# Transposing both halves of a head's numerators in one visit, with a second PSUM bank and new planner rules

## The chip, the cores and the metric

The kernel runs on one core of a Trainium2 chip. The metric is the device time of one execution in microseconds, as the median of several runs. A profiled execution gives the trace that is read below. Of the core's engines, TensorE (PE) does matrix products and transposes into PSUM, a small memory of eight banks; VectorE (DVE) and ScalarE (ACT) do elementwise work and empty the banks; GpSimd (POOL) and SyncE (SP) issue DMAs, and ACT issues some too. Each engine runs its own instructions strictly in order, and waits on semaphores for the others.

## The reference

One block of a streaming encoder: 1024 frames with 16 learned tokens ahead of them, model width 1024. Four mLSTM heads and four retention heads are mixed in parallel, then comes a gated MLP with a causal convolution (width 2816). Cut to what matters here:

```python
h = concat(meta, x)                                   # 1040 x 1024
proj = rmsnorm(h) @ w_in                              # q, k, v, output gate, input and forget gates of all heads
# per head (8 heads: 4 mLSTM, 4 retention; q, k 128 wide, v 256 wide), chunk by chunk:
num = (q k^T * decays) v + (q * decay) C              # C is the state carried from chunk to chunk
C   = decay * C + k^T v
h_head = head_norm(num) * g                           # normalised over the head's 256 values
mixed = [sigmoid(o) * h_head | silu(o) * h_head]      # gated, 2048 wide
h = h + mixed @ w_out
h = h + (silu(conv(rmsnorm(h) @ w_up)) * (rmsnorm(h) @ w_gate)) @ w_down
out = rmsnorm(h)
```

## The kernel before

**Products.** Large products are done in a seven-product scheme (Strassen and Winograd). Each operand is split into a high and a low part of type fp32r, and a product is three matmuls: high by high, low by high, high by low (`mm3s`, lines 900 to 902). Everything that belongs to the scan over the chunks (scores `s`, state update `u`, numerator `n`, transposes) is done in plain fp32 instead. So TensorE changes between fp32r and fp32 operands each time the scan gets a turn.

**Stages.** The input is normalised and the first projections made (0 to about 85 us of the trace). Then, head by head in the order 4, 0, 1, 2, 3, 5, 6, 7, come the products of the queries and keys (`q`), the values (`vp`, for a pair of heads; `v` for head 7) and the output gate (`o`). The scan of one head is woven into the products of the following one, up to about 712 us. Then come the output projection (`pw` tiles), the MLP (`up`, `ga`) and the down projection (`pd`). The change touches the weaving between 85 and 712 us.

**The scan of a head.** There are nine chunks (one of 16 tokens, eight of 128), and `scan_a` and `scan_b` handle one each. `scan_a` makes the scores and transposes the keys in the PSUM bank `sA`. `scan_b` makes the state update `u` in the bank `upd` (line 1568), the numerator `n` in the bank `num` (1570, 1572), adds `u` to the state `C` on DVE (1581) and copies the numerator out on ACT (1583). The chunks are grouped in three pieces (`PIECES`: chunks 0 to 3, 4 to 6, 7 and 8). When a piece is normalised (`stats`), its numerators, 256 wide, are transposed in two halves of 128: `half(b)` (line 1623) puts up to four transposes into the one bank `tr` (1629), and DVE multiplies them by the gain and the gate into an SBUF tile `mx` (1637). Three `mx` buffers rotate (1647). For the last piece DVE also copies two columns (1652). Then ACT issues a DMA that stores `mx` to DRAM (1655). Head 7 writes into the operand tiles `wa` of the output projection instead and stores nothing. So a head has six visits of `half`, each between two groups of product matmuls.

**The order of the work is planned when the program is built.** A function `watch` (line 132) sees every instruction, keeps a modelled clock for each engine and pins the order of PE, DVE and ACT between 85 and 712 us. A change between fp32r and fp32 on PE is costed there at 0.1 us (line 178). The products are cut into steps of 12 matmuls for a bank; `slot` (1701) issues a step, and after it takes tasks from the front of a list `side` (the scan, the transposes, the gates), strictly in order, as long as the first one's condition holds. Conditions look at `done`: a key stands there with the modelled time at which it becomes true, and holds when PE's modelled clock has passed it. `half` needs the piece's `z`, the gate's half `sig` and `tr`, which is taken out when the transposes are issued and put back after the multiplication on DVE. A task runs up to its first `yield`; `tick` continues it later. `settle` makes the DMA wait until the planner's clock has passed the modelled end of what came before. `drain` issues what is left of the list at the end of a stage without steps between.

How many tasks a step may take is set by a table `RULES`, with an entry for the seven products of a kind at one of their places, such as `("q", 1)`. Its seven numbers are: how many weight units ahead are treated as near; a slack in us before a waiting task is continued; by how many us DVE or ACT may be ahead of PE before waiting tasks are held back; the same limit for taking new tasks; the most tasks in a step; the order of the queues; the most PE tasks in a step. The clock, the DMA model and the conditions stay as they are.

```python
c += 0.1 * (whole != kindof[0])                       # line 178: the change of operands
tr = ps.tile([P, 512], F32, tag="tr", name=f"tr{h}_{p}_{b}")
mx = mxp.tile([P, WMAX], F32, tag="mx", name=f"mx{h}_{p}_{b}", bufs=3)
yield from settle()
AC.dma_start(mxd[i][:, a0 - MA:e - MA], mx[:, :e - a0])
```

## Time and profile before

| what | before |
|---|---|
| median of 3 runs | 1527.99 us (1526.26 to 1529.33) |
| profiled execution | 1527.2 us, of which the span from first to last instruction is 1525.4 us |
| PE busy | 1489.9 us, 98% of the span |
| DVE busy | 1090.1 us, 71% |
| ACT busy | 755.6 us, 50% |
| granted TensorE clock | 0.994 |

In the timeline a row is one group of instructions: start in us from the span's beginning, duration in us, engine, line, operation, what it writes and reads, shape, count, and in brackets how long its engine sat idle before it and who ended that. PE means matmuls (their ends are modelled, so two rows overlap; the distance of their starts is what they cost). In a table of waits a row is: who waited, for whom, us in total, times, longest. An engine with q behind its name is its sequencer, which issues DMAs.

### The profile page before, as it was taken

The numbers are of one execution on the slowest core, as the hardware profiler recorded it, in microseconds if no ns is written. First come the engines' busy times: TensorE is split into PE (matmuls) and PEld (weight loads), VectorE is DVE, ScalarE is ACT, GpSimd is POOL, SyncE is SP. The second block draws the span as 40 slices with busy tenths as digits, with TensorE's granted clock in tenths as the row PEclk, the third lists the DMA queues.
The fourth block names the chain that finished last, engine by engine and source line by source line (L and its number), as shares of the span: only waits on it lengthen the run. The fifth ranks groups of instructions, "written<-read, shape, count | busy, mean of one in ns | idle before, by whom it ended". The sixth has DMA issues, their size and how long they took to land.

```text
span 1525.4 us, 25488 instructions
## 1 busy us (share of the span) xinstructions
PE 1489.9 (98%) x9929; PEld 1350.0 (88%) x9929; DVE 1090.1 (71%) x2087; ACT 755.6 (50%) x1453; POOL 73.6 (5%) x153
## 2 busy tenths in 40 slices
PE   6999999999999999999999999999999999999997
PEld 6998999999999999986888988999999999888887
DVE  7785868678777677856867787767666666778657
ACT  4465655554655455553454565444444444444443
POOL 1000000000000000000000001222220000000000
PEclk9999999999999999999999999999999999999999
DMA  6022255323532355696333247888772224933313
GB/s 232 8 88 51 86 159 194 111 82 114 186 119 98 125 166 189 195 398 255 111 112 134 80 124 241 197 208 200 189 183 77 83 79 160 369 105 110 97 42 111
DMA packets 104586, 223.81 MB, mean 147 GB/s; under 512 B 10520, under 2 KB 33760, under 8 KB 104288
## 3 DMA queue, kind: packets, MB, share of 16 engines
q1 hardware_dynamic: 89824, 191.68, 37.7%
q0 software_dynamic: 8448, 23.07, 7.6%
q10 hardware_dynamic: 6192, 7.41, 1.4%
q8 instruction: 78, 1.28, 0.4%
q14 instruction: 44, 0.36, 0.1%
HBM read 178.05 MB, written 67.15 MB: 161 GB/s over the span
## 4 chain that ended last, share of the span: by engine, by line
PE 89%; DVE 6%; DMA 2%; ACT 2%; issue 1%; SPq 0%; DVEq 0%; ACTq 0%
PE pdx L902 3%; PE pdx L901 3%; PE pdx L900 3%; PE pup_x L901 2%; PE pup_x L902 2%; PE pga_x L900 2%; PE pup_x L900 2%; PE pga_x L901 2%; PE pga_x L902 2%; PE pdy L902 2%; PE pdy L901 2%; PE pdy L900 2%; PE n L1570 2%; PE pwx L902 2%; PE u L1568 2%; PE pv L940 2%
## 5 line engine op out<-in xcount | busy, mean ns | idle before, releaser
L780 ACT CAST hi_up<-raw_up 128x512 fp32r<-128x512 f32 (+1 forms) x52 | 36.4, 719 | 107.4 <-PE pga_z L901 61.1
L781 DVE TENSOR_TENSOR lo_ga<-fraw_ga,hi_ga 128x512 fp32r<-128x512 f32 (+1 forms) x52 | 41.9, 809 | 37.3 <-ACT hi_ga L780 37.1
L781 DVE TENSOR_TENSOR lo_up<-raw_up,hi_up 128x512 fp32r<-128x512 f32 (+1 forms) x52 | 41.3, 810 | 38.0 <-ACT hi_up L780 37.2
L900 PE MATMUL pup_x<-uh_g,hi_up 128*128 128x256 f32 (+1 forms) x240 | 67.2, 282 | 1.2 <-ACT uh_g L1928 1.2
L901 PE MATMUL pup_x<-ul_g,hi_up 128*128 128x256 f32 (+1 forms) x240 | 67.4, 282 | 0.1
L902 PE MATMUL pup_x<-uh_g,lo_up 128*128 128x256 f32 (+1 forms) x240 | 66.4, 282 | 0.0
L781 DVE TENSOR_TENSOR lo_d<-rd,hi_d 128x1024 fp32r<-128x1024 f32 (+1 forms) x34 | 37.7, 1114 | 32.8 <-ACT hi_d L780 32.7
L780 ACT CAST hi_ga<-fraw_ga 128x512 fp32r<-128x512 f32 (+1 forms) x52 | 36.4, 719 | 45.3 <-PE pup_z L901 21.9
L902 PE MATMUL pdx<-uh_d,lo_d 128*128 128x512 f32 (+1 forms) x156 | 57.9, 375 | 0.0
L901 PE MATMUL pdx<-ul_d,hi_d 128*128 128x512 f32 (+1 forms) x156 | 57.8, 374 | 0.0
L780 ACT CAST hi_d<-rd 128x1024 fp32r<-128x1024 f32 (+1 forms) x34 | 32.3, 959 | 49.3 <-PE pdy L901 32.5
L902 PE MATMUL pdy<-uh_d,lo_d 128*128 128x512 f32 x132 | 51.9, 393 | 0.0
L901 PE MATMUL pdy<-ul_d,hi_d 128*128 128x512 f32 x132 | 51.7, 392 | 0.0
L900 PE MATMUL pdx<-uh_d,hi_d 128*128 128x512 f32 (+1 forms) x156 | 48.5, 372 | 0.0
L900 PE MATMUL pdy<-uh_d,hi_d 128*128 128x512 f32 x132 | 47.9, 389 | 0.0
L900 PE MATMUL pga_x<-uh_g,hi_ga 128*128 128x512 f32 x120 | 47.5, 396 | 0.0
L901 PE MATMUL pga_x<-ul_g,hi_ga 128*128 128x512 f32 x120 | 47.5, 396 | 0.0
L900 PEld LDWEIGHTS pup_x<-uh_g,hi_up 128*128 128x128 f32 x240 | 45.3, 189 | 2.3 <-ACT uh_g L1928 1.4
L902 PE MATMUL pga_x<-uh_g,lo_ga 128*128 128x512 f32 x120 | 47.1, 393 | 0.0
L901 PEld LDWEIGHTS pup_x<-ul_g,hi_up 128*128 128x128 f32 x240 | 45.4, 189 | 1.0 <-DVE ul_g L1929 0.3
L902 PEld LDWEIGHTS pup_x<-uh_g,lo_up 128*128 128x128 f32 x240 | 44.8, 189 | 0.8
L1637 DVE SCALAR_TENSOR_TENSOR mx<-tr,vec,sig 128x386 f32<-128x386 f32 (+2 forms) x42 | 24.0, 572 | 20.7 <-PE tr L1629 16.0
(1684 smaller groups left out, 5752.4 us busy)
## 6 DMA issues: line engine op xcount, KB each, us to landing
raw_up<-w_up_d SPq DMA_DIRECT2D x22, 512.0 KB, 4.4
fraw_ga<-w_gate_d SPq DMA_DIRECT2D x22, 512.0 KB, 4.1
acts<-cv SPq DMA_DIRECT2D x44, 256.0 KB, 4.2
wsd<-w_down_d POOLq DMA_DIRECT2D x44, 256.0 KB, 6.6
rd<-wsd SPq DMA_DIRECT2D x22, 512.0 KB, 3.6
raw_w<-w_out_d SPq DMA_DIRECT2D x20, 512.0 KB, 6.8
wsw<-raw_w SPq DMA_DIRECT2D x32, 256.0 KB, 3.7
raw_m<-w_out_d SPq DMA_DIRECT2D x14, 512.0 KB, 4.0
```

The source lines that it names most:

```text
L780: AC.copy(hi[:, o:o + n], x)
L781: V.tensor_tensor(lo[:, o:o + n], x, hi[:, o:o + n].bitcast(F32), ALU.subtract)
L900: m.append(PE.matmul(pt, ah, xh_, start=first and k == 0, stop=False, skip_group_check=True))
L901: PE.matmul(pt, ah, xl_, start=False, stop=False, skip_group_check=True)
L902: m.append(PE.matmul(pt, al, xh_, start=False, stop=last and k == n - 1, skip_group_check=True))
L940: PE.matmul(pv[:, :nv], u[:, kb % 4, j0:j0 + L], (w0hi, w0lo)[j][kb // 4][:, o:o + nv], start=i + j + kb == 0, stop=i == 1 and kb == KB - ...
L1568: PE.matmul(up[:, :nv], kw[:L], v, start=True, stop=True)
L1570: PE.matmul(pn[:L, :nv], pt[:L, :L], v, start=True, stop=c == 0)
L1637: return V.scalar_tensor_tensor(dst, tr[:, x0 - t0:x1 - t0], vec[:, g:g + 1], sig(b, p)[:, x0 - a0:x1 - a0], ALU.mult, ALU.mult)
```

## The change

The two visits `half(0)` and `half(1)` of a piece become one, `both`. It takes two banks: `tr` for the first half and `upd`, the bank of the state updates, for the second. It issues the transposes of both halves (up to eight) one behind the other. At its continuation DVE does the two multiplications one behind the other, each freeing its bank, and for the last piece the small copies; after one common `settle`, ACT issues the two stores together. Its condition asks for `tr` and `upd` and for both halves of the gate. Since `upd` now has two users, `scan_b` takes it out of `done` before the update and puts it back when the state has been made, and its condition asks for it. The `mx` buffers stay three.

In the planner, the change of operands costs 0.13 us instead of 0.1, and 17 of the 19 entries of `RULES` are other numbers. One `drain` keeps 3 tasks instead of 4 back for head 6, since a piece is one task now.

```diff
-    ("o", 0): (4, 0.3, 3.0, 2.5, 2, 0, 3),
+    ("o", 0): (4, 0.3, 3.0, 2.5, 4, 0, 2),
...
-    ("o", 7): (2, 0.5, 3.0, 2.5, 1, 0, 1),
-    ("q", 0): (3, 0.3, 2.0, 1.5, 3, 0, 3),
-    ("q", 1): (2, 0.5, 3.0, 1.5, 3, 1, 1),
+    ("o", 7): (4, 0.5, 3.0, 4.0, 2, 0, 1),
+    ("q", 0): (3, 0.8, 2.0, 1.5, 2, 0, 3),
+    ("q", 1): (4, 0.3, 4.5, 1.5, 3, 1, 1),
...
-                c += 0.1 * (whole != kindof[0])
+                c += 0.13 * (whole != kindof[0])
...
         if c < NCH - 1:
+            done.discard("upd")
             up = pp(f"u{h}_{c}", "upd")
...
             state["C"] = C
+            done.add("upd")
...
-        def half(b):
+        def both():
             num = m["num"]
             done.discard("tr")
-            tr = ps.tile([P, 512], F32, tag="tr", name=f"tr{h}_{p}_{b}")
-            for i, c in enumerate(chs):
-                c0, L = CH[c]
-                PE.transpose(tr[:, c0 - t0:c0 - t0 + L], num[i][:L, b * P:(b + 1) * P], ident[:L, :L])
+            done.discard("upd")
+            tr = [ps.tile([P, 512], F32, tag=x, name=f"{x}{h}_{p}") for x in ("tr", "upd")]
+            for b in range(2):
+                for i, c in enumerate(chs):
+                    c0, L = CH[c]
+                    PE.transpose(tr[b][:, c0 - t0:c0 - t0 + L], num[i][:L, b * P:(b + 1) * P], ident[:L, :L])
             yield
...
+            for b in range(2):
...
+                mx = mxp.tile([P, WMAX], F32, tag="mx", name=f"mx{h}_{p}_{b}", bufs=3)
+                mix_into(mx[:, :w], a0, t1)
+                done.add(("tr", "upd")[b])
+                if e < t1:
+                    V.tensor_copy(mm[:, i], mx[:, e - a0:w])
+                    posted.add(i)
+                out.append((i, mx))
             yield from settle()
-            AC.dma_start(mxd[i][:, a0 - MA:e - MA], mx[:, :e - a0])
-            stored.add((i, p))
+            for i, mx in out:
+                AC.dma_start(mxd[i][:, a0 - MA:e - MA], mx[:, :e - a0])
+                stored.add((i, p))
...
-            return lambda: (h, c) in pre and done.can(("pre", h, c), *(turn if c == 0 else [("n", h, c - 1)] + v))
+            return lambda: (h, c) in pre and done.can(("pre", h, c), *(turn if c == 0 else [("n", h, c - 1)] + v), *(["upd"] if c < NCH - 1 else []))
...
-    done["tr"] = 0.0
+    done["tr"] = done["upd"] = 0.0
...
-        drain(f"sig{a}", 4)
+        drain(f"sig{a}", 4 if b < H else 3)
```

## The prediction

> **What bounds the kernel now.** I read the page's engine shares first, then the busy times by stage, then TensorE's waits in the one stage that the change touches.

> ```profile
> span 1525.4 us, 25488 instructions
> PE 1489.9 (98%) x9929; PEld 1350.0 (88%) x9929; DVE 1090.1 (71%) x2087; ACT 755.6 (50%) x1453; POOL 73.6 (5%) x153
> PE 89%; DVE 6%; DMA 2%; ACT 2%; issue 1%; SPq 0%; DVEq 0%; ACTq 0%
> ```

> PE is busy for 98% and carries 89% of the chain that ended last. So time is won only by taking work from PE or by closing its gaps. The busy times by stage, from the start of the planned order to its end (busy us and instructions of PE, PEld, DVE, ACT, POOL; then clock, DMA share, GB/s):

> ```profile
> 85.00:170.00 85.00, 80.99 (x617) 77.23 (x616) 58.92 (x147) 50.63 (x103) 0.53 (x5) 0.98 0.24 69
> 170.00:250.00 80.00, 77.45 (x606) 72.35 (x605) 58.83 (x139) 42.59 (x93) 2.41 (x14) 1.00 0.48 146
> 410.00:650.00 240.00, 239.87 (x1896) 227.90 (x1896) 178.79 (x390) 131.81 (x276) 1.93 (x12) 1.00 0.45 147
> 650.00:712.00 62.00, 58.53 (x351) 48.89 (x350) 36.26 (x80) 29.52 (x58) 0.00 (x0) 0.99 0.93 350
> sum 627.00, PE 615.74 PEld 576.11 DVE 450.04 ACT 342.47 POOL 9.13; mean PE 102.62 PEld 96.02 DVE 75.01 ACT 57.08 POOL 1.52
> ```

> PE stands idle for 627.0 - 615.7 = 11.3 us of 627. That is all a better order can win, unless the visits themselves become cheaper. From 410 to 650 us there is nothing to win: 0.13 us idle in 240. TensorE's waits between 85 and 712 us (total, times, longest):

> ```profile
> PE s L1523 <- DVE pt L1547: 2.6, 1, 2.6
> PE pwy L901 <- DVE wr L1288: 1.8, 1, 1.8
> PE u L1568 <- DVE C L1581: 1.5, 2, 0.9
> PE tr L1629 <- DVE mx L1637: 1.5, 3, 1.1
> PE pwy L900 <- ACT wr L1288: 1.3, 1, 1.3
> PE pe L1240 <- DVE gsm L1236: 0.8, 1, 0.8
> PE pe L1239 <- DVE gates L1232: 0.6, 1, 0.6
> PE s L1523 <- DVE pt L1542: 0.6, 1, 0.6
> ```

> They fall into four groups: waits for the bank `tr`, 1.5; the tail where the output projection begins (`pwy`), 1.8 + 1.3 = 3.1; other waits of the scan, 2.6 + 1.5 + 0.6 = 4.7; the gates, 0.8 + 0.6 = 1.4. No row has a product waiting for its bank to be emptied.

> **Term 1, the visits saved: 0.** Eight heads with six visits each become 24 visits instead of 48, so 24 pairs of changes between fp32r and fp32 go. What does one cost? Three visits, PE's timeline (distances of starts):

> ```profile
> 230.10 0.28 PE L902 MATMUL pq1x<-uS2h,lo_q 128*128 128x264 f32 x1
> 230.31 0.23 PE L1629 MATMUL tr<-cs,vz 16*128 16x16 f32 x1
> 230.47 0.55 PE L1629 MATMUL tr<-cs,v 128*128 128x128 f32 x3
> 230.97 0.28 PE L901 MATMUL pq1y<-uS1l,hi_q 128*128 128x264 f32 x1
> 234.28 0.29 PE L902 MATMUL pq1y<-uS1h,lo_q 128*128 128x264 f32 x1
> 234.41 0.49 PE L1629 MATMUL tr<-cs,v 128*128 128x128 f32 x3
> 234.86 0.28 PE L901 MATMUL pq1x<-uS3l,hi_q 128*128 128x264 f32 x1
> 234.98 0.28 PE L902 MATMUL pq1x<-uS3h,lo_q 128*128 128x264 f32 x1
> 237.85 0.28 PE L902 MATMUL pq1x<-uS3h,lo_q 128*128 128x264 f32 x1
> 237.97 0.38 PE L1629 MATMUL tr<-cs,v 128*128 128x128 f32 x2
> 238.32 0.28 PE L901 MATMUL pq1y<-uS4l,hi_q 128*128 128x264 f32 x1
> ```

> A product matmul follows the one before after 234.98 - 234.86 = 0.12. From the last product matmul ahead of a visit to the second one behind it there would be 2 x 0.12 = 0.24 without the visit. With three transposes it is 234.86 - 234.28 = 0.58, so the visit costs 0.34; with two it is 238.32 - 237.85 = 0.47, so 0.23. The difference, 0.11, is the price of one transpose. Three times 0.11 is 0.33, twice is 0.22: 0.01 is left for going in and coming out. The planner's 0.1, now 0.13, for each of the two changes is not in the trace. 24 x 0.01 is 0.2, which I round to 0, with bounds of -0.5 and +0.5.

> The first piece begins with a chunk of 16 tokens. Its visit costs 230.97 - 230.10 - 0.24 = 0.63 for four transposes, 0.19 more than 4 x 0.11. That goes with the change from 128 rows to 16 and back. In the merged visit the order is 16, 128, 128, 128, 16, 128, 128, 128: four changes of shape, as in two visits. So 0 again. [...]

> **Term 2, the bank `tr`: -1.5.** Today the second half waits for the first to be multiplied; with a second bank it need not. The 1.5 us go, at best with the pipeline's restart (-1.9); the low end is 0, if the next piece waits instead. `upd` costs nothing: tasks leave the list strictly in order, a head's last update (chunk 7) lies ahead of its transposes, and the next head's first update behind them. No instruction of PE, DVE or ACT is added or dropped; the stores stay 42.

> **Term 3, the tail: -1.5.** The last two visits, of head 7, and what follows on PE and DVE:

> ```profile
> 704.05 0.38 PE L1629 MATMUL tr<-cs,n 128*128 128x128 f32 x2
> 706.35 0.38 PE L1629 MATMUL tr<-cs,n 128*128 128x128 f32 x2
> 711.40 0.80 PE L901 MATMUL pwy<-wr,hi_w 128*128 128x512 f32 x1 [1.78 <-DVE wr L1288]
> 705.36 0.48 DVE L1637 SCALAR_TENSOR_TENSOR wa<-tr,vec,sig 128x254 f32<-128x254 f32 x1
> 708.41 0.48 DVE L1637 SCALAR_TENSOR_TENSOR wa<-tr,vec,sig 128x254 f32<-128x254 f32 x1
> 710.66 0.69 DVE L1288 TENSOR_TENSOR wr<-wa,wr 128x512 fp32r<-128x512 f32 x1
> ```

> The multiplication at 708.41 is in DVE's queue ahead of the split `wr`, for which PE waits. Its visit came 2.30 us behind the first half's, at the end of all product steps. In one visit both come at 704.05 or earlier, the more so as the last rule of the stage, ("o", 7), allows a limit of 4.0 instead of 2.5 and two tasks in a step instead of one. The split then starts earlier by at least the 0.48 and the small copy behind it; I take 1.5 of the 3.1 us. Ends: -3.1, all of it, and +0.7, where the pair itself is left to the end and a second 0.48 with its copy stands ahead of the split.

> **Term 4, the order drawn anew: -1.0.** 17 rules change, so the place of nearly every task moves. I can't work out the new order from the trace. Of the 4.7 us of other waits, 2.6 is a single event (124 us); an order with a wait there is not the usual one, since 240 us went by without any. So I expect a part of it to go: -1.0, with ends -4.7 (all) and +4.7 (as much again). The gates' 1.4 stays.

> **Term 5, three `mx` buffers for pairs: +0.5.** The views of the tile `mx` and of the chain:

> ```profile
> L1637 DVE SCALAR_TENSOR_TENSOR mx<-tr,vec,sig x42: 476/613/622, 149.9 to 632.8; 128x386 f32<-128x386 f32 x14, 128x384 f32<-128x384 f32 x14, 128x256 f32<-128x256 f32 x14
>   DMA mxd<-mx: 1.9, 2
> DMA to landing us min/median/max: 2.0/3.1/6.0
> ...
> 235.80 4.42 DMA mxd<-mx
> ...
> 240.34 0.48 DVE L1637 SCALAR_TENSOR_TENSOR mx<-tr,vec,sig 128x256 f32<-128x256 f32 x1 [1.36 <-DMA mxd<-mx]
> 240.88 0.44 PE L1629 MATMUL tr<-cs,v 128*128 128x128 f32 x2 [1.07 <-DVE mx L1637]
> ```

> A store needs 2.0 to 6.0 us to land. Today DVE waited twice for a buffer (1.9 us, of which 1.36 became 1.07 on PE). In pairs, the second half of a piece needs the buffer of the first half of the piece before, and that buffer's store is issued only behind both multiplications (one more 0.61) and the common `settle`. So the wait gets likelier. In today's two cases the smaller one (1.9 - 1.36 = 0.5) stopped nothing; I add 0.5 on PE, between 0 and the +9 of the second rival.

> **Sum.** 0 - 1.5 - 1.5 - 1.0 + 0.5 = -3.5 us. The profiled execution took 1527.2 us (1.8 outside the span) and comes to 1523.7; the median shown, 1527.99, is 0.8 above it and comes to 1524.5. I forecast 1524.5.

> **The rivals.**
> - *The change of operands does cost what the planner says.* Then 24 x 2 x 0.13 = 6.2 us more go: 1518.3. For it speaks only that PE is the bound; against it the 0.01 left over above.
> - *The pairs wait for their stores (slower).* The place is DVE's multiplication of the next piece, with PSUM banks of the products to be emptied queued behind it. Visits of one head followed each other by 1.8 (two visits in 237.97 - 234.41) to 2.9 us (240.88 - 237.97). In pairs the stores go out behind 0.7 of transposes, 1.2 of multiplications and what ACT has queued, so some 3 us after the visit began, and land by 9 if they take the longest 6.0 seen; the next piece's second multiplication is due at about 2.9 + 0.7 + 1.2 = 5. DVE then stands for up to 4 us. Three heads at 3 and four heads at nothing make +9; with terms 3 and 4 (-2.5) and the present 1.5 given back, that is 1527.99 - 2.5 - 1.5 + 9 = 1533. It decides from 3.1 + 4.0 = 7.1 us of such waits on. For it: the 1.36 today. Against it: median landing of 3.1. [...]
> - *The new order loses as much again.* Looser rules let DVE fall behind in other places: 1527.99 + 4.7 = 1532.7. For it: DVE is busy 450 of 627 us and now gets two multiplications (1.2 us) at once. Against it: nothing waits for an emptied bank today.

> **Chances.** Forecast (-7 to 0): 0.45. Changes dear: 0.10. Pairs wait: 0.25, of which about two thirds end slower. Order loses: 0.20, half of it slower. What a measurement of this kernel can tell from no change is about 0.2%, 3.1 us. Forecast gives 0.26 faster and 0.19 same; dear changes 0.10 faster; the pairs 0.07 same and 0.18 slower; the order 0.04 faster, 0.04 same, 0.12 slower. Together 0.40, 0.30, 0.30. The likeliest case alone spans 1521 to 1528; the range reaches from the first rival to the second, 1517.5 to 1534.

> **What would show it.** Term 1: a merged visit of six transposes costs 0.66 us, of eight with 16 rows 1.26. Term 2: no row of `tr` waiting for `mx`. Term 3: head 7's last transposes before 704, `pwy` waiting less than 3.1 in all. Term 4: idle of PE in the 627 us near 8. Term 5: DVE's wait of `mx` for stores near today's 1.9. I am wrong if a merged visit is clearly below the sum of its transposes, or if that DVE wait is several us and PE waits behind it.

## The result, and the profile after

The changed kernel takes 1530.39 us (median, 1527.27 to 1534.2), the kernel before 1528.05 us in the same comparison. The ratio is 1.0017, 95% interval 1.001 to 1.0024: slower by 0.17%, where 0.2% faster was forecast. The time lies inside the forecast range, but the sign is the other one, and 1 lies outside the interval. The profiled execution took 1528.65 us, 1526.9 of it the span.

The page of the changed kernel, engine shares and chain:

```profile
PE 1491.4 (98%) x9929; PEld 1352.4 (89%) x9929; DVE 1089.0 (71%) x2087; ACT 756.5 (50%) x1454; POOL 73.6 (5%) x153
PE 83%; DVE 7%; DMA 6%; ACT 2%; issue 1%; SPq 0%; DVEq 0%; ACTq 0%
```

No instruction of PE or DVE came or went (9929 and 2087). ACT has one more (1454 for 1453, a table load of 1.28 us), which the prediction had excluded. DMA has grown from 2% to 6% of the chain, but a second profile of the same kernel (after_again, below) has 3%, so nothing is built on that here. The busy times by stage (columns as in the prediction):

```profile
...
650.00:712.00 62.00, 60.84 (x385) 52.46 (x384) 34.88 (x80) 31.26 (x64) 0.00 (x0) 1.00 1.00 374
sum 627.00, PE 615.44 PEld 576.20 DVE 444.00 ACT 343.40 POOL 9.09; mean PE 102.57 PEld 96.03 DVE 74.00 ACT 57.23 POOL 1.52
```

PE stands idle for 627.0 - 615.4 = 11.6 us, as long as before (11.3). That hides two opposite changes. The same view cut at 700 us, first of the kernel before:

```profile
85.00:700.00 615.00, 606.98 (x4682) 569.67 (x4681) 439.05 (x1005) 339.43 (x706) 9.13 (x58) 1.00 0.46 152
700.00:720.00 20.00, 16.77 (x61) 12.73 (x60) 14.01 (x23) 4.89 (x7) 0.00 (x0) 0.83 0.67 236
```

and of the changed kernel:

```profile
85.00:700.00 615.00, 603.53 (x4669) 566.64 (x4658) 436.38 (x1002) 338.32 (x706) 9.09 (x58) 1.00 0.44 148
700.00:720.00 20.00, 19.91 (x92) 16.10 (x91) 15.31 (x26) 7.38 (x11) 0.00 (x0) 1.00 0.96 359
```

Up to 700 us PE's idle time grew from 8.0 to 11.5 us. From 700 to 720 us it fell from 3.2 to 0.1, and there the granted clock rose from 0.83 to 1.00. The waits of TensorE in the changed kernel, 85 to 712 us:

```profile
PE s L1523 <- DVE pt L1542: 3.7, 3, 2.6
PE s L1523 <- DVE pt L1547: 2.0, 2, 1.8
PE pv0x L901 <- DVE lo_vp L479: 1.2, 1, 1.2
PE pq0x L900 <- DVE sig L972: 1.1, 1, 1.1
PE po7x L902 <- DVE lo_o L479: 0.9, 1, 0.9
...
PE upd L1633 <- DVE mx L1644: 0.2, 1, 0.2
```

The waits of `pwy` are gone and those for `mx` nearly. (`pt` is the scores `s` after DVE has multiplied them; the next scores wait for that.) Three rows are of a new kind: products wait, once for a bank to be emptied (`pq0x` for `sig`) and twice for an operand's low part (`lo_vp`, `lo_o`).

The span in five parts, worked out from the starts of four groups in the timelines: head 4's output gate (`po4`), head 7's (`po7`), the first sum of columns behind the output projection (`pcb`), the down projection (`pd`). The scan runs from `po4` to `po7`, the tail from `po7` to `pcb`. All kernels of the experiments are in it, in us of the profiled execution. Between the same starts PE has the same number of matmuls in every kernel (4391 in the scan, 962 in the tail), so no column grows because work moved into it:

| kernel | to po4 | scan | tail | pcb to pd | rest | ratio to before (95%) |
|---|---|---|---|---|---|---|
| before | 76.2 | 568.1 | 190.3 | 463.0 | 227.8 | 1 |
| before_again | 76.9 | 567.9 | 189.1 | 464.6 | 227.8 | |
| after | 77.7 | 571.9 | 184.9 | 464.6 | 227.8 | 1.0017 (1.001 to 1.0024) |
| after_again | 76.0 | 574.0 | 185.0 | 464.6 | 227.8 | |
| rules_only | 76.3 | 576.2 | 187.2 | 463.8 | 227.8 | 1.0023 (1.0013 to 1.0033) |
| price01 | 76.9 | 571.9 | 184.9 | 464.6 | 227.8 | 1.0017 (1.0009 to 1.0026) |
| split_mix | 76.9 | 578.2 | 184.5 | 463.1 | 227.8 | 1.0049 (1.0037 to 1.0061) |
| after_free | 75.7 | 574.1 | 184.9 | 464.6 | 227.8 | 1.0019 (1.001 to 1.0028) |
| merge5 | 77.1 | 574.6 | 182.9 | 464.0 | 227.8 | 1.0004 (0.9995 to 1.0012) |
| merge57 | 76.3 | 574.8 | 182.9 | 463.9 | 227.8 | 1.001 (1.0 to 1.0019) |
| merge57_free | 75.9 | 573.8 | 182.9 | 463.9 | 227.8 | 0.9998 (0.9988 to 1.0008) |
| merge7 | 76.9 | 568.5 | 182.9 | 466.3 | 227.8 | 0.9969 (0.9957 to 0.9981) |
| rule7 | 77.8 | 568.5 | 184.8 | 464.6 | 227.8 | 0.9981 (0.9973 to 0.999) |
| merge7_rule | 77.1 | 567.6 | 184.1 | 466.1 | 227.8 | 0.997 (0.9961 to 0.9979) |

The change made the scan longer by 4 to 6 us and the tail shorter by 4 to 5. The column `pcb to pd` is not touched by any kernel here; it differs by up to 3.3 us between executions, for a reason that comes at the end.

### The profile page after: what moved, and what is told of

Same layout as the page of the kernel before. It is cut to its first block, busy times and chain, and to the rows that moved or that the text cites. A ratio compares the mean times of both kernels' runs of the same rounds, so it can differ in the third digit from the quotient of the medians.

```text
span 1526.9 us, 25471 instructions
## 1 busy us (share of the span) xinstructions
PE 1491.4 (98%) x9929; PEld 1352.4 (89%) x9929; DVE 1089.0 (71%) x2087; ACT 756.5 (50%) x1454; POOL 73.6 (5%) x153
## 3 DMA queue, kind: packets, MB, share of 16 engines
q8 instruction: 78, 1.28, 0.4%
## 4 chain that ended last, share of the span: by engine, by line
PE 83%; DVE 7%; DMA 6%; ACT 2%; issue 1%; SPq 0%; DVEq 0%; ACTq 0%
PE pdx L902 3%; PE pdx L901 3%; PE pdx L900 3%; PE pup_x L901 2%; PE pup_x L900 2%; PE pup_x L902 2%; PE pga_x L900 2%; PE pga_x L901 2%; PE pga_x L902 2%; PE pdy L902 2%; PE pdy L901 2%; PE pdy L900 2%; PE pwx L902 2%; PE pwx L900 2%; PE pwx L901 2%; PE n L1571 2%
## 5 line engine op out<-in xcount | busy, mean ns | idle before, releaser
L900 PE MATMUL pup_x<-uh_g,hi_up 128*128 128x256 f32 (+1 forms) x240 | 67.5, 284 | 1.2 <-ACT uh_g L1936 1.2
L901 PE MATMUL pup_x<-ul_g,hi_up 128*128 128x256 f32 (+1 forms) x240 | 67.6, 283 | 0.1
L902 PE MATMUL pup_x<-uh_g,lo_up 128*128 128x256 f32 (+1 forms) x240 | 66.5, 283 | 0.0
L902 PE MATMUL pdx<-uh_d,lo_d 128*128 128x512 f32 (+1 forms) x156 | 57.9, 375 | 0.0
L901 PE MATMUL pdx<-ul_d,hi_d 128*128 128x512 f32 (+1 forms) x156 | 57.8, 374 | 0.0
L902 PE MATMUL pdy<-uh_d,lo_d 128*128 128x512 f32 x132 | 51.9, 393 | 0.0
L901 PE MATMUL pdy<-ul_d,hi_d 128*128 128x512 f32 x132 | 51.7, 392 | 0.0
L900 PE MATMUL pdx<-uh_d,hi_d 128*128 128x512 f32 (+1 forms) x156 | 48.5, 372 | 0.0
L900 PE MATMUL pdy<-uh_d,hi_d 128*128 128x512 f32 x132 | 47.9, 389 | 0.0
L900 PEld LDWEIGHTS pup_x<-uh_g,hi_up 128*128 128x128 f32 x240 | 45.6, 190 | 2.3 <-ACT uh_g L1936 1.4
L900 PE MATMUL pga_x<-uh_g,hi_ga 128*128 128x512 f32 x120 | 47.5, 396 | 0.0
L901 PE MATMUL pga_x<-ul_g,hi_ga 128*128 128x512 f32 x120 | 47.5, 396 | 0.0
L902 PE MATMUL pga_x<-uh_g,lo_ga 128*128 128x512 f32 x120 | 47.1, 393 | 0.0
L901 PEld LDWEIGHTS pup_x<-ul_g,hi_up 128*128 128x128 f32 x240 | 45.6, 190 | 1.0 <-DVE ul_g L1937 0.3
L902 PEld LDWEIGHTS pup_x<-uh_g,lo_up 128*128 128x128 f32 x240 | 45.0, 190 | 0.8
L660 POOL DMA_DIRECT2D wsd<-w_down_d x33 | 19.3, 697 | 381.0 <-DVE s2up L2164 377.8
```

Of the source, the lines that this page charges most:

```text
L660: dep(G.dma_start(x, y), last["pace"], True)
L900: m.append(PE.matmul(pt, ah, xh_, start=first and k == 0, stop=False, skip_group_check=True))
L901: PE.matmul(pt, ah, xl_, start=False, stop=False, skip_group_check=True)
L902: m.append(PE.matmul(pt, al, xh_, start=False, stop=last and k == n - 1, skip_group_check=True))
```

## Experiments

**The two kernels once more.** The kernel before and the changed kernel, unaltered.

> The kernel before once more, for a second profile. Order theory (the new order of the scan loses, the tail gains): TensorE idles about 11 us of the 627 from 85 to 712 us as in the first profile, with the 3 us at the output projection's beginning among it. Half-speed theory (windows of half clock after a wait are part of the cost and fall differently in each execution): a window of half clock lies again near 710 us, behind the two waits there, while the other windows may move; the sum at half speed differs from the first profile's 21.4 us by one or more steps of 3.4.

> The changed kernel once more, for a second profile. Half-speed theory: its first profile (span 1526.9) lay below its median because few of the scan's waits were followed by a window of half clock; this one has one to three windows more between 85 and 712 us and a longer span, 1527 to 1531. If the windows stand where they stood and the span is within 0.5 us of 1526.9, the windows don't explain why the median is 1530.4.

The scan repeats for the kernel before (567.9) and is again longer in the changed one (574.0). So the two columns differ by more than executions do: 0.2 us between the two of before, 2.1 between the two of after.

In before_again PE idles 10.9 us of the 627, and the waits of `pwy` are there again (1.8 and 1.3 us). Of the 6.83 us at clock 0.50 that stood at 710.76 us in the first profile, 3.41 are left (at 712.23), and a stretch of 3.41 has come at 920.44. So the time at half clock is nearly the same (20.8 us after 21.4), where a difference in steps of 3.4 was expected. In after_again one stretch has come in the scan: the 3.41 us from 269.99, right behind a wait of 2.68 us for `pt`, ran at clock 0.50. The first profile of the changed kernel has none there. That costs 1.7 of the 2.1 us by which its two scans differ.

**Only the new rules.** The kernel before, with `half` as it was, the 17 new rules and the price of 0.13.

```diff
-    ("o", 7): (2, 0.5, 3.0, 2.5, 1, 0, 1),
+    ("o", 7): (4, 0.5, 3.0, 4.0, 2, 0, 1),
...
-                c += 0.1 * (whole != kindof[0])
+                c += 0.13 * (whole != kindof[0])
```

> The new rules and the price of 0.13, with two visits a piece and one bank as before. Order theory: the scan loses as in the changed kernel, since the rules move the tasks; 1528 to 1533. Pairs theory (two multiplications one behind the other and stores issued together hold DVE): the loss goes, DVE's wait for stores is back near 1.9 us from 8.4, and the kernel is faster than before, 1523 to 1526.

Measured: 1530.09 us, ratio 1.0023. The loss is there without any merged visit. DVE's wait for stores, expected near 1.9 us if the pairs caused it, is 6.1 us in this profile, so it grows without pairs:

```profile
DVE mx L1637 <- DMA mxd<-mx: 6.1, 3, 2.4
```

TensorE's waits of rules_only, 85 to 712 us:

```profile
PE s L1523 <- DVE pt L1547: 5.0, 4, 3.0
...
PE pv0x L901 <- DVE lo_vp L479: 1.2, 1, 1.2
PE pq0x L900 <- DVE sig L972: 1.1, 1, 1.1
PE po7x L902 <- DVE lo_o L479: 0.9, 1, 0.9
```

The last three stand in rules_only with the very durations of the changed kernel, and so they do in after_again, price01 and after_free. Neither before nor merge7 nor rule7, which keep the old rules for the scan, has any of them. Together they are 3.2 us, of the 3.5 by which the changed kernel's idle time up to 700 us grew; its other waits went up (`pt`, 3.2 to 5.7) and down (`tr`, 1.5 to 0.2; `C`, 1.5 to 0.5) and come to about nothing. `po7x` waits at 659.94 us, behind the start of `po7`, so its 0.9 us count in the tail. The other two, 2.3 us, are most of what PE's idle time in the scan column grew by: 8.4 us in before, 11.0 in after. It is 12.4 in after_again and 13.7 in rules_only, whose waits for `pt` are longer. How two of the three come about is seen in DVE's timeline of the changed kernel:

```profile
101.56 0.69 DVE L479 TENSOR_TENSOR lo_q<-raw_q0a,hi_q 128x512 fp32r<-128x512 f32 x1
...
104.09 0.41 DVE L972 TENSOR_TENSOR sig<-sig,po4y 128x256 f32<-128x256 f32 x1
...
155.56 0.62 DVE L1644 SCALAR_TENSOR_TENSOR mx<-upd,vec,sig 128x386 f32<-128x386 f32 x1
156.09 1.28 DVE L479 TENSOR_TENSOR lo_vp<-raw_vp,hi_vp 128x512 fp32r<-128x512 f32 x2
...
268.04 0.69 DVE L565 TENSOR_TENSOR raw_q2b<-raw_q2b 128x512 f32<-128x512 f32 x1 [3.28 <-DMA raw_q2b<-w_g_d]
...
704.96 0.47 DVE L1644 SCALAR_TENSOR_TENSOR wa<-upd,vec,sig 128x254 f32<-128x254 f32 x1
```

and the matmuls that waited, with the merged visits of 309 and 311 us, in PE's timeline of the changed kernel:

```profile
104.56 0.39 PE L900 MATMUL pq0x<-u11h,hi_o 128*128 128x264 f32 x1 [1.14 <-DVE sig L972]
...
156.83 0.39 PE L901 MATMUL pv0x<-lo_vp,uS2h 128*128 128x256 f32 x1 [1.19 <-DVE lo_vp L479]
...
270.04 0.49 PE L1523 MATMUL s<-qT,kT 128*128 128x128 f32 x2 [2.57 <-DVE pt L1542]
...
308.80 0.28 PE L902 MATMUL pv1x<-hi_vp,u11l 128*128 128x256 f32 x1
309.01 0.23 PE L1633 MATMUL tr<-cs,vz 16*128 16x16 f32 x1
...
310.31 0.28 PE L901 MATMUL pv1x<-lo_vp,u11h 128*128 128x256 f32 x1
...
311.50 0.29 PE L902 MATMUL pv1x<-hi_vp,u11l 128*128 128x256 f32 x1
311.62 0.49 PE L1633 MATMUL tr<-cs,v 128*128 128x128 f32 x3
311.95 0.49 PE L1633 MATMUL upd<-cs,v 128*128 128x128 f32 x3
...
312.40 0.28 PE L901 MATMUL pv1x<-lo_vp,u11h 128*128 128x256 f32 x1
```

At 104 us DVE empties a bank of `po4y` into `sig` only after a split (`lo_q`) and three operations of the rotary embedding; in the kernel before that copy ran at 100.05, ahead of them:

```profile
100.05 0.41 DVE L972 TENSOR_TENSOR sig<-sig,po4y 128x256 f32<-128x256 f32 x1
```

At 157 us the split `lo_vp` stands behind the two multiplications of a piece. In rules_only it stands behind one (155.95 us), and the wait is the same 1.19 us, so it doesn't take a pair. At 270 us a product's weights landed late (DVE stood 3.28 us for them) and the scan's `pt` was queued behind them. None is long, but each time DVE ran first what stood ahead in its queue, and PE stood for 1.14, 1.19 and 2.57 us.

**The old price.** The changed kernel with 0.1 in place of 0.13.

```diff
-                c += 0.13 * (whole != kindof[0])
+                c += 0.1 * (whole != kindof[0])
```

> The changed kernel with the planner's price of a change of operands back at 0.1 instead of 0.13; all else as in it. If the price matters only through the order it draws, the time moves by no more than the scan's waits do, 1527 to 1533, with no sign that can be told beforehand. If the dearer price is itself what makes the plan worse (PE's modelled clock runs later than the chip's), the waits of PE in the scan shrink and it is at 1526 or below.

Measured: 1529.71 us, ratio 1.0017, that of the changed kernel; scan and tail are equal to it within 0.1 us. The order is almost the same too: of PE's 9929 matmuls 7 stand at another place. Under the new rules the dearer change of operands plays no part.

**Each half by itself behind the merged transposes.** The changed kernel, but the first half is multiplied, settled and stored before the second is multiplied.

```diff
-            out = []
...
-                out.append((i, mx))
-            yield from settle()
-            for i, mx in out:
+                yield from settle()
                 AC.dma_start(mxd[i][:, a0 - MA:e - MA], mx[:, :e - a0])
```

> The changed kernel, but after the common visit of TensorE each half is multiplied, settled and stored by itself, as before. Pairs theory: DVE's wait for stores falls from 8.4 and 4.2 us to about 2, and the time by 2 to 4 us to 1526 to 1528. Order theory: the time stays within the spread that new orders have, 1528 to 1533, since the wait at the stores reached TensorE only in part.

Measured: 1534.61 us, ratio 1.0049, the slowest of all and above both forecasts. DVE's wait for stores in it, 85 to 712 us, is a single one of 1.3 us. Two of TensorE's waits:

```profile
PE po6y L902 <- DVE lo_o L479: 2.4, 1, 2.4
PE po3y L902 <- DVE lo_o L479: 1.6, 1, 1.6
```

The wait for stores is far below the 8.4 us of the changed kernel, and the time is worse. The edit also redraws the order, and the new order has late splits `lo_o` in two more places. So fewer waits for stores alone don't make the kernel faster; as the order changed with them, this run doesn't tell the two apart.

**The waits for stores taken away.** The changed kernel in the same order of instructions; the second halves of the middle pieces of heads 5 and 6 go to an area that is idle by then (`um`, in which two small tiles, `ug` and `mask`, are joined). The planner keeps the times it had for `mx`, and PE, DVE and ACT run the same instructions in the same order as in the changed kernel.

```diff
                 mx = mxp.tile([P, WMAX], F32, tag="mx", name=f"mx{h}_{p}_{b}", bufs=3)
+                if h in (5, 6) and (p, b) == (1, 1):
...
+                    mx = um
```

> The changed kernel in its own order; only the second halves of the middle pieces of heads 5 and 6 are written into an idle area, so the two waits of DVE for a store at 563 and 635 us (2.4 us each in the changed kernel's trace) go. If the pairs' waits for their stores are what makes the changed kernel's scan longer, the scan (first output-gate product of head 4 to that of head 7) falls from 572 to 574 us by 2 us or more and the time to 1527 or below. If the order drawn anew is the cause, TensorE reached only 0.3 us of these waits: the scan stays at 571 to 574 us and the time within 0.5 us of 1530.

Measured: 1530.02 us, ratio 1.0019; the scan takes 574.1. DVE's wait for stores fell from 8.4 to 3.5 us, and nothing came of it. The two waits taken away (2.4 us each) were only 0.2 and 0.5 us in after_again, whose scan is as long (574.0), so they come and go between executions without setting the time.

Most of what is left is one wait, 2.75 us at 240.88 us (2.71 at 240.73 in the changed kernel). It could still delay DVE up to the late weights of 270 us. split_mix tells against that: there the same multiplication starts at 240.96 without a wait, the weights are late all the same, and PE waits 1.4 and 1.1 us for `pt` at 268 and 273 us. DVE's timeline of split_mix:

```profile
240.96 0.61 DVE L1643 SCALAR_TENSOR_TENSOR mx<-upd,vec,sig 128x384 f32<-128x384 f32 x1
...
266.13 0.69 DVE L565 TENSOR_TENSOR raw_q2b<-raw_q2b 128x512 f32<-128x512 f32 x1 [4.14 <-DMA raw_q2b<-w_g_d]
```

**Only head 7's pieces merged.** The kernel before with old rules; `both` for head 7, `half` for all others. The order is the old one up to there.

```diff
+        if h != 7:
+            return [(stats, ...)] + [(lambda b=b: half(b), ...) for b in range(2)]
+        return [(stats, ...), (both, ...)]
```

> The rules and the price of before; only head 7, which stores nothing, transposes both halves in one visit. The order up to head 7 is that of before. If the gain at the tail comes from the merged visit, the waits at the output projection (3.1 us) and the window of half clock behind them (up to 3.4) go: 1522 to 1526. If it needs the new rule of the last products too, the tail stays: 1527.5 to 1528.5.

Measured: 1522.36 us, ratio 0.9969 (0.9957 to 0.9981), the fastest of all: faster than the kernel before and the changed one. Its busy times from 700 us:

```profile
700.00:720.00 20.00, 20.00 (x88) 16.34 (x87) 18.26 (x25) 8.69 (x12) 0.00 (x0) 1.00 0.70 243
```

No idle time, and full clock. The tail falls by 7.4 us against the profiled execution of before and by 6.2 against before_again; the scan stays (568.5).

**Only the rule of the last stage, and both together.**

```diff
-    ("o", 7): (2, 0.5, 3.0, 2.5, 1, 0, 1),
+    ("o", 7): (4, 0.5, 3.0, 4.0, 2, 0, 1),
```

> The kernel before with one rule changed, that of the last products ("o", 7), to its new numbers; two visits a piece. If looser limits alone bring head 7's transposes forward, the tail's waits and its half-speed window go as in the kernel that merges head 7: 1522 to 1524. If the merged visit is what it takes, 1526 to 1528.

> Rules and price of before with head 7 in one visit, and the last products' rule ("o", 7) at its new numbers: the two changes that each took the tail's waits, together. Both close the same waits, so the gains don't add up: 1521 to 1524.5, no better than the better of the two by more than 1. If they did add (0.31% and 0.19%): 1520.

The rule alone, on the kernel before: 1524.35 us, ratio 0.9981, just above the range for a gain by the rule. With head 7 merged as well: 1523.29, ratio 0.997, no better than merging alone. Both remove the same wait, so their gains don't add.

**More heads merged under the old rules.** First heads 4, 1, 3, 5 and 7 (merge5), then 5 and 7 (merge57). The edits against the kernel with head 7 alone:

```diff
-        if h != 7:
+        if h not in (4, 1, 3, 5, 7):      # merge5; (5, 7) in merge57
```

> The rules and the price of before, both halves in one visit for heads 4, 1, 3, 5 and 7; heads 0, 2 and 6 as before. Four heads more than in the kernel with head 7 alone (1522.4), so 12 visits fewer. If a change of operands costs what the planner says, 12 x 0.2 = 2.4 to 12 x 0.26 = 3.1 us more go: about 1519.5. If it costs nothing and pairs do no harm: 1521 to 1524. If pairs that wait for their stores are what the changed kernel loses by: DVE's wait for stores rises from 2.6 us towards 8 and the time to 1525 to 1527.

> Rules and price of before, one visit a piece for heads 5 and 7. In the kernel with five merged heads, head 5's pair held DVE 3.6 us for a store, and TensorE then waited 2.9 and 1.3 us at the products po6. Pairs theory: head 5 alone brings both back, 4 us over the kernel with head 7 alone: 1526 to 1528. Order theory: the order behind head 5 is drawn anew but needn't hold that wait: 1522 to 1526, and if the wait is there without DVE having stood for a store, the order is the cause.

Measured: 1527.75 (1.0004) and 1528.63 (1.001), each above every range that was forecast for it. One more head than in merge7 gives away all that head 7 gained: the scan goes from 568.5 to 574.8. merge5 merges three more heads, loses by the same two waits and takes no longer (scan 574.6), so the pairs of heads 4, 1 and 3 neither gain nor cost. TensorE's two largest new waits in merge57:

```profile
PE po6x L902 <- DVE lo_o L479: 2.9, 1, 2.9
...
PE po6y L902 <- DVE lo_o L479: 1.3, 1, 1.3
```

DVE's timeline of merge57 shows head 5's pair waiting for a store, and the late split:

```profile
559.04 0.62 DVE L1644 SCALAR_TENSOR_TENSOR mx<-upd,vec,sig 128x384 f32<-128x384 f32 x1 [3.48 <-DMA mxd<-mx]
...
572.94 0.68 DVE L479 TENSOR_TENSOR lo_o<-raw_o6a,hi_o 128x512 fp32r<-128x512 f32 x1
```

and its busy times in steps of 3.41 us show the clock:

```profile
570.75:574.16 3.41, 0.49 (x5) 0.48 (x5) 3.38 (x6) 2.15 (x5) 0.00 (x0) 1.00 0.58 227
574.16:577.57 3.41, 3.41 (x19) 3.41 (x18) 3.37 (x8) 0.89 (x2) 0.00 (x0) 0.50 0.53 154
577.57:580.99 3.42, 2.43 (x13) 1.30 (x12) 2.83 (x7) 1.58 (x4) 0.00 (x0) 1.00 0.26 66
580.99:584.40 3.41, 3.08 (x14) 3.08 (x15) 0.27 (x1) 0.39 (x1) 0.00 (x0) 0.50 0.22 88
```

Each of the two waits comes with a stretch of 3.41 us at half clock, 1.7 us lost each; the second begins 0.33 us before its wait ends (581.32). Waits and stretches make at most 2.9 + 1.3 + 2 x 1.7 = 7.6 us; the scan grew by 6.3 against merge7. Here the rival of the pairs was alive again: a wait of 3.48 us for a store, and DVE without a gap from there to the split that PE waits for. The next run takes that wait out.

**merge57 without the wait for the store.** The same order of instructions; head 5's middle piece writes its second half to the idle area.

```diff
+                if (h, p, b) == (5, 1, 1):
+                    mx = um
```

> Heads 5 and 7 merged with the old rules, in the same order of instructions as merge57; only the second half of head 5's middle piece is written into an area that is idle by then, so it waits for no store. In merge57 DVE stood 3.5 us there (559 us), then ran without a gap until the late conversion lo_o, for which TensorE waited 2.9 and 1.3 us (574 and 581 us), each behind or ahead of a half-clock window. If the wait for the store is the cause (the rival of the pairs), DVE is 3.5 us earlier, both waits of po6 and both windows go, and the time falls by 4.2 + 1.7 to 3.4 us to some 1521 to 1523, the level of merge7. If the order itself puts the conversions too late, the two waits stay near 2.9 and 1.3 and the time is that of merge57, 1527 to 1529.

Measured: 1527.76 us, ratio 0.9998. TensorE's waits of merge57_free:

```profile
PE po6x L903 <- DVE lo_o L480: 2.5, 1, 2.5
...
PE po6y L903 <- DVE lo_o L480: 1.3, 1, 1.3
```

and its DVE timeline:

```profile
554.55 0.61 DVE L1645 SCALAR_TENSOR_TENSOR um<-upd,vec,sig 128x384 f32<-128x384 f32 x1
555.86 0.41 DVE L973 TENSOR_TENSOR rawk<-rawk,pq6x 128x248 f32<-128x248 f32 x1 [0.71 <-PE pq6x L903]
557.33 0.43 DVE L973 TENSOR_TENSOR rawk<-rawk,pq6x 128x264 f32<-128x264 f32 x1 [1.05 <-PE pq6x L903]
558.72 0.43 DVE L973 TENSOR_TENSOR rawk<-rawk,pq6y 128x264 f32<-128x264 f32 x1 [0.96 <-PE pq6y L903]
```

The 3.48 us are gone, but DVE then stands for the products of `pq6` instead, 0.71 + 1.05 + 0.96 = 2.7 us: the operation behind the pair needs a product that isn't ready yet. The pair's first half begins 0.93 us earlier than in merge57 (554.01 for 554.94) and the split `lo_o` 1.46 (571.48 for 572.94), so half a microsecond is won; PE still waits 2.5 and 1.3 us, and both half-clock stretches stay (573.6 and 580.5 us). The order of DVE's queue sets most of this, and not the store. The time is where the theory of the order put it. The ratio is 0.0012 lower than that of merge57 (1.8 us), with intervals that overlap, so a share of up to about 2 us for the store isn't excluded.

## Why the prediction was wrong

**Term 1 (visits saved: 0) was right.** The prediction asked for 0.66 us for six transposes and 1.26 for eight with 16 rows. Measured, as distances of starts less 0.24: 312.40 - 311.50 - 0.24 = 0.66, and 310.31 - 308.80 - 0.24 = 1.27. Merging visits buys nothing on TensorE, and the rival of the dear change of operands falls. The 1.27 is twice the 0.63 of one set with 16 rows, so the extra 0.19 is paid for each set, in one visit as in two; what it consists of the runs don't show.

**Term 2 (bank `tr`: -1.5) was right in kind, not in each execution.** 0.2 us were left in the profiled execution, 1.4 in after_again, 2.0 in price01. The low end of the forecast, that the next piece waits instead, does occur.

**Term 3 (tail: -1.5) was mis-sized.** It is -5.4 us in the profiled executions (190.3 to 184.9) and -4.1 in the repeats. The mechanism was as put: the last multiplication came at 704.96 in place of 708.41, the `pwy` waits went whole, 3.1 us. But `po7x` now waits 0.9, so PE's idle time in the tail column fell by 2.3 us (3.5 to 1.2). What wasn't seen is that the wait also cost clock. In the kernel before the clock was 0.83 over the 20 us from 700, that is 20 x 0.17 = 3.4 us of full speed lost; in before_again it was 0.91, 1.8 us. The stage view read for the prediction ended at 712 us, before most of that stretch, and its 0.99 was taken for nothing. merge7 and rule7 show that this term alone is worth 0.2 to 0.3%.

**Term 4 (the order drawn anew: -1.0) is the step that failed.** The sign was wrong: the scan became 3.8 (571.9 - 568.1) to 6.1 us (574.0 - 567.9) longer. That is the third rival, "the new order loses as much again", and its +4.7 was near. The reason given for it, looser rules that let DVE fall behind, is what the three new waits show, though the prediction gave it 0.20 since "nothing waits for an emptied bank today". The forecast argued that 240 us without a wait make waits unusual. But that was one order's property, not the planner's: the scan takes 572 to 578 us in each kernel here whose order was drawn anew in it (after, rules_only, price01, split_mix, merge5, merge57), against 568 in the old one. Redrawing cost 4 to 10 us each time. These aren't six independent draws: price01 has nearly the order of after, and merge5 and merge57 lose by the same two waits, while the pairs of heads 4, 1 and 3 in merge5 cost nothing. So a loss is likely where an order is redrawn, but not bound to come. No kernel here merges all eight heads under the old rules, so what that would bring is open.

**Term 5 (three buffers: +0.5) was right on PE and wrong on DVE.** The view of the tile `mx` in the changed kernel:

```profile
  DMA mxd<-mx: 8.4, 4
...
DMA to landing us min/median/max: 2.0/2.8/7.5
```

DVE's wait rose from 1.9 to 8.4 us (4.2 in after_again), above the 7.1 from which the second rival was to decide. It did not decide: PE met 0.2 us of it as a wait of `upd`, and after_free shows that taking more than half of it away changes nothing. Nor does the rise need pairs: rules_only has 6.1 us.

**The sum.** In the two profiled executions the scan's +3.8 and the tail's -5.4 make -1.6 us; the parts of the span that the change doesn't touch add 1.5 (76.2 to 77.7) and 1.6 (463.0 to 464.6), and the spans differ by +1.5. The repeats give 6.1 - 4.1 = +2.0 for scan and tail. Part of this spread is the clock: PE's idle time alone gives 2.6 - 2.3 = +0.3 and 4.3 - 2.3 = +2.0. So the stages explain a result between -1.6 and +2.0 us, and the interval of the ratio says +1.5 to +3.7. The two meet only at their edge. What fills the rest is open; it may be which executions happened to be profiled.

Two slips of the prediction changed little: half of the third rival's 0.20 is entered as 0.12, and the 0.4 us of restarts in term 2's best case (-1.9) come from no row. In the changed kernel the matmul behind the wait that ends at 156.83 us is followed by the next after 0.22 us in place of 0.12, which would make 0.3 for three waits.

## What to carry to other kernels

Merge visits to an engine for what they free, not for what changing over is thought to cost: read first from distances of starts whether the change has a price. When an edit makes a planner redraw an order, compare the kernel with only the order redrawn; here that alone made the scan 8.1 us longer (rules_only), and the most that merging took off the tail was 7.4. The same idea applied only where the wait stood (merge7: one head of eight, old order elsewhere) gave 0.31%.

## What the runs showed of the hardware

Over all 14 profiled executions, from 60 to 1500 us, PE idles 1.89 us or more in 18 steps of the grid, and half clock follows every one of them (in the kernel before 2.20 us from 120.26 and 1.97 from 707.35). Of the 37 steps with 1.30 to 1.88 us it follows 16 (in the changed kernel 1.82 us from 122.23 and the 1.33 from 917.54, but not 1.53 from 265.59). Of the 124 with 0.5 to 1.3 us it follows 6. No step is idle throughout: the most is 3.41 - 0.49 = 2.92 us, from 570.75 in merge57. And in merge57 PE is busy for 2.43 of the 3.42 us from 577.57, and the next step is at half clock all the same. So the idle time within one step matters, but it doesn't decide alone.
